# A two-layer decoder trunk: the first layer's first MLP matrix as seven block products over both token halves

## The chip, the cores and the metric

The kernel runs on one core of one Trainium2 chip. The metric is the device time of one execution in microseconds; lower is better. All numbers of the profile come from one profiled execution of the same program.

## The reference

1024 tokens of width 1024 in float32 pass two layers. Layer 0 is an mLSTM (8 heads, chunks of 128 tokens) and an MLP; layer 1 is a latent attention (8 heads, causal, rotary keys and queries) on keys and values that are computed once from the stream after layer 0, and an MLP. Each part is wrapped in two RMS norms and modulated by six vectors that are products of the condition `c` with large matrices. What matters here:

```python
def sqrelu_mlp(h, w1, w2):
    return jnp.square(jax.nn.relu(h @ w1)) @ w2          # w1 (1024, 4096), w2 (4096, 1024)

def rope_tables(positions):
    half = B_ROPE // 2
    inv = ROPE_THETA ** (-jnp.arange(half, dtype=jnp.float32) / half)
    ang = positions.astype(jnp.float32)[..., None] * inv
    return jnp.cos(ang), jnp.sin(ang)
...
        h = modulate(rmsnorm(x, norm_g[l, 2]), sh2, sc2)
        y = sqrelu_mlp(h, mlp_w1[l], mlp_w2[l])
```

## The kernel before

The tokens are handled in two halves of 512 (`hfs[0]`, `hfs[1]`). The stream is kept transposed, features on partitions, so that a block of 128 features and one half is a tile of 128x512. Every float32 product is three matmuls in a reduced format: each operand is split in a high and a low part, and `mm3` (L268) adds low x high, high x low and high x high. For weights, `wload` (L244) reads 512 KB into one of 4 `raw` buffers through SyncE's DMA queue, and `wsplit` (L223) makes the high part with ScalarE (L228) and the low part with VectorE (L229), in two of 8 `ws` buffers. Operands are split in the same way by `split_mod` (L479).

Buffers go by kind: 24 tiles of 128x1024 (`k4`), 8 (`hd`), 8 (`ws`), 4 (`raw`), and smaller ones of 128x512 (3 `tmp`, 6 `tmc`). [...]

*MLP.* `mlp` (from L937) makes a list of steps for one half. A hidden step makes one of 32 blocks of 128 hidden features: 8 k-tiles of `w1`, 24 matmuls of 512 columns, then relu, square and split. An up step multiplies a group of hidden blocks by a part of `w2`, 24 matmuls too, and VectorE adds the result to `y` (`accumulate`). Loads run two steps ahead (`AHEAD`). For the second half of layer 1 alone, pairs of hidden blocks are made by seven block products instead of eight (`hidden_pair`), over the two quarters of that half's tokens.

*Order of the work.* The order is written by hand with generators. `two_streams` runs a dense stream (an MLP) beside another (an attention, or background work): the other yields how many dense steps are to follow; each dense step can also advance a third stream, the background (`fill`), which makes the modulation vectors on VectorE (`ada_chunk`, L374), the rotary tables (`rope_tables`, L1182 and around) and the folded latent weights (`latent_weights`, L1260). Layer 0's MLP of the first half runs beside the second half's norms and this background; that of the second half beside the attention of the first (`mixer1(hfs[0], ...)`, with `attention_first`, which prepares two heads at a time and then attends with them); layer 1's MLP of the first half beside the attention of the second. Before that, `in_turn` weaves a half's output projection (`wout`) with the other half's chunks, and `post` makes the residual and the MLP's input. A scheduler then orders each engine's instructions by the program's priorities, by readiness in its own timeline and by free buffers; at run time each engine's queue is in that order.

The lines that the prediction names: L229, L237 (the adds of `accumulate`), L270 to L272 (`mm3`), L905 (the reload of x for the residual), L926 (its use), L980 (a block sum in `hidden_pair`), L1182 and L1260, L1462 to L1466 (softmax), L301 and L715 (what GpSimd does now).

## Time and profile before

| | |
|---|---|
| median of 3 runs | 2344.38 us (2344.23 to 2345.63) |
| the profiled execution, from first to last instruction | 2341.8 us |
| TensorE busy | 2316.1 us (99%), 12234 matmuls |
| VectorE busy | 1661.9 us (71%) |
| ScalarE busy | 1097.5 us (47%) |
| GpSimd busy | 17.8 us (1%) |
| DMA | 373.02 MB, mean 159 GB/s |

The page gives busy time by engine, the chain of work that ended last, and groups of instructions: line, engine, operation, output and inputs, shapes and count; then busy time in us and mean ns of one; then the engine's idle time ahead of them with what ended it. The view by stretches gives, for a stretch of the span, its length, each engine's busy time with its count, the TensorE clock, the DMA engines' busy share and GB/s. The profiled execution's own time outside the span isn't recorded; the median is 2.6 us above the span.

### The profile page before, as it was taken

To read this page: it belongs to the slowest core of one execution; us is meant where nothing else is said; L and a number is where in the kernel's file an instruction comes from. 1 tells how busy PE (TensorE), PEld (TensorE's weight loads), DVE (VectorE), ACT (ScalarE), POOL (GpSimd) and SP (SyncE) were. 2 spreads that over 40 slices of the span, in tenths; PEclk is the share of its full clock that TensorE was granted. 3 is DMA by queue.
4 is the path that set the end of the run, shared out by engine and by line. 5 is a ranking of instruction groups with operands and counts; after the bars stand their busy time and mean duration, and the time that the engine had idled before them with its cause. 6 is when DMAs were issued, how large, how long until landed. Compare 5 with 4: busy or idle time off the path is not lost.

```text
span 2341.8 us, 32190 instructions
## 1 busy us (share of the span) xinstructions
PE 2316.1 (99%) x12234; PEld 1957.3 (84%) x12234; DVE 1661.9 (71%) x2643; ACT 1097.5 (47%) x1825; POOL 17.8 (1%) x95
## 2 busy tenths in 40 slices
PE   8999999999999999999999999999999999999998
PEld 6888888888888887888888888888888888989997
DVE  6666766868665768777764867765666488788776
ACT  4364335655333454444444554444444444655543
POOL 1000000000000000000000000000000000000000
PEclk9999999999999999999999999999999999999999
DMA  9543454545653845545543454873433452455432
GB/s 319 176 130 121 145 160 142 171 148 167 189 181 114 274 156 167 170 158 179 173 137 119 153 162 154 261 245 132 153 100 129 123 166 81 145 157 163 134 108 108
DMA packets 377595, 373.02 MB, mean 159 GB/s; under 512 B 24323, under 2 KB 284480, under 8 KB 377440
## 3 DMA queue, kind: packets, MB, share of 16 engines
q1 hardware_dynamic: 377152, 370.86, 50.0%
q8 instruction: 96, 1.57, 0.3%
q14 instruction: 59, 0.48, 0.1%
q0 software_dynamic: 288, 0.10, 0.0%
HBM read 312.19 MB, written 58.72 MB: 158 GB/s over the span
## 4 chain that ended last, share of the span: by engine, by line
PE 90%; DVE 4%; DMA 3%; ACT 2%; issue 1%; SPq 0%; DVEq 0%; ACTq 0%
PE ps L270 15%; PE ps L272 15%; PE ps L271 15%; PE pm L270 10%; PE pm L271 10%; PE pm L272 10%; PE pc L270 2%; PE pc L272 2%; PE pc L271 2%; PE pc L1572 1%; DMA raw<-in_mlp_w_dram 1%; PE pm L1458 1%; DVE wl L229 1%; PE pm L812 1%; PE pm L1452 1%
## 5 line engine op out<-in xcount | busy, mean ns | idle before, releaser
L229 DVE TENSOR_TENSOR wl<-raw,wh 128x1024 fp32r<-128x1024 f32 (+3 forms) x367 | 437.9, 1197 | 303.2 <-ACT wh L228 291.9
L228 ACT CAST wh<-raw 128x1024 fp32r<-128x1024 f32 (+3 forms) x367 | 376.8, 1030 | 559.8 <-PE ps L270 218.3
L270 PE MATMUL ps<-k,wl 128*128 128x512 f32 (+1 forms) x1432 | 546.4, 382 | 2.1 <-DVE wl L229 2.1
L272 PE MATMUL ps<-k,wh 128*128 128x512 f32 (+1 forms) x1432 | 539.2, 377 | 0.0
L271 PE MATMUL ps<-k,wh 128*128 128x512 f32 (+1 forms) x1432 | 538.3, 376 | 0.0
L270 PEld LDWEIGHTS ps<-k,wl 128*128 128x128 f32 x1432 | 270.0, 189 | 53.9 <-DVE wl L229 4.0
L272 PEld LDWEIGHTS ps<-k,wh 128*128 128x128 f32 x1432 | 269.7, 188 | 49.4 <-issue 0.2
L271 PEld LDWEIGHTS ps<-k,wh 128*128 128x128 f32 x1432 | 270.1, 189 | 47.8 <-issue 1.4
L237 DVE TENSOR_TENSOR k<-k,pm 128x512 f32<-128x512 f32 (+1 forms) x278 | 226.1, 844 | 81.1 <-PE pm L272 80.4
L270 PE MATMUL pm<-hd,wl 128*128 128x512 f32 x512 | 201.3, 393 | 0.5 <-ACT hd L483 0.5
L271 PE MATMUL pm<-hd,wh 128*128 128x512 f32 x512 | 199.5, 390 | 0.2 <-DVE hd L484 0.2
L272 PE MATMUL pm<-hd,wh 128*128 128x512 f32 x512 | 199.4, 390 | 0.0
L270 PE MATMUL pm<-wh,hd 128*128 128x512 f32 x488 | 193.7, 397 | 4.2 <-ACT raw L1464 2.7
L272 PE MATMUL pm<-wh,hd 128*128 128x512 f32 x488 | 190.6, 390 | 0.0
L271 PE MATMUL pm<-wl,hd 128*128 128x512 f32 x488 | 190.6, 390 | 0.0
L374 DVE SCALAR_TENSOR_TENSOR tma<-raw,cond,tma 128x512 f32<-128x512 f32 x168 | 125.6, 747 | 21.3 <-DMA raw<-in_kv_ada_w_dram 13.4
L1464 ACT ACTIVATE raw<-pm,sm 128x128 f32<-128x128 f32 (+3 forms) x64 | 47.4, 741 | 150.6 <-DVE sm L1463 122.3
L484 DVE TENSOR_TENSOR hd<-tmp,hd 128x512 fp32r<-128x512 f32 x128 | 88.1, 689 | 39.5 <-ACT hd L483 39.0
L270 PEld LDWEIGHTS pm<-hd,wl 128*128 128x128 f32 x512 | 96.2, 188 | 21.2 <-ACT hd L483 0.9
L270 PEld LDWEIGHTS pm<-wh,hd 128*128 128x128 f32 x488 | 91.8, 188 | 26.1 <-ACT raw L1464 5.1
L271 PEld LDWEIGHTS pm<-hd,wh 128*128 128x128 f32 x512 | 96.2, 188 | 20.4 <-DVE hd L484 0.5
L272 PEld LDWEIGHTS pm<-hd,wh 128*128 128x128 f32 x512 | 96.2, 188 | 19.9
(430 smaller groups left out, 3995.4 us busy)
## 6 DMA issues: line engine op xcount, KB each, us to landing
raw<-in_mlp_w_dram SPq DMA_DIRECT2D x256, 512.0 KB, 4.3
raw<-in_ada_w_dram SPq DMA_DIRECT2D x80, 512.0 KB, 4.5
raw<-in_a_w_in_dram SPq DMA_DIRECT2D x44, 512.0 KB, 4.6
xs<-k SPq DMA_DIRECT2D x40, 256.0 KB, 4.5
raw<-in_a_w_out_dram SPq DMA_DIRECT2D x16, 512.0 KB, 5.1
raw<-in_kv_ada_w_dram SPq DMA_DIRECT2D x16, 512.0 KB, 3.9
kd<-k SPq DMA_DIRECT2D x32, 256.0 KB, 3.9
vd<-k SPq DMA_DIRECT2D x32, 256.0 KB, 4.7
```

The source lines that it names most:

```text
L228: nc.scalar.copy(hi[:, :n], r[:, :n])
L229: i = nc.vector.tensor_sub(lo[:, :n], r[:, :n], hi[:, :n].bitcast(F32))
L237: return f(*a, **k)
L270: nc.tensor.matmul(o, ll, rh, start=start, stop=False)
L271: nc.tensor.matmul(o, lh, rl, start=False, stop=False)
L272: pe_last[0] = nc.tensor.matmul(o, lh, rh, start=False, stop=stop)
L374: nc.vector.scalar_tensor_tensor(acc, r[:, kk], cond[:, k : k + 1], acc, ALU.mult, ALU.add)
L484: nc.vector.tensor_sub(lo, u, hi.bitcast(F32))
L812: nc.tensor.matmul(nvs[q][:, r, i], hf.PT[p_][:, r, cs], v[2 * p_ + r], start=g == 0, stop=True,)
L1452: nc.tensor.matmul(o[:, :w], ql, kh, start=True, stop=False)
L1458: nc.tensor.matmul(o[:, :w], qh, kh, start=False, stop=True)
L1464: nc.scalar.activation(pr[:, :n], f, AF.Exp, bias=m, scale=SCALE, accum_out=l)
```

## The change

Layer 0's MLP gets a class of its own, `Mlp`, that works on both halves. `w1` is a 2x2 matrix of blocks (input features 0-511 and 512-1023, hidden features 0-2047 and 2048-4095), the tokens are the two halves; seven block products replace eight. Sixteen pairs of hidden blocks (p, p + 16) go through three sweeps. Sweep 1 makes two products per pair: the first half's hidden block p; one product is stored (`m`). Sweep 2 makes three: the first half's block p + 16; two partial sums are stored (`u`). Sweep 3 makes two: both hidden blocks of the second half. Sweeps 1 and 2 run where the first half's MLP ran, sweep 3 beside the first half's attention. `post` of the second half makes the operands that the block products need, from the first half's MLP input, which is kept in memory (`keep`).

The sums of weight blocks (`t0`) are made early, during layer 0's mLSTM, by `block_sums`: all 16 pairs are in its order; what the steps around it haven't taken by the end of the second half's projections is issued in one block there. The low parts of `w2` are stored when the first half makes them and read back for the second half.

```diff
     def mm3(o, lh, ll, rh, rl, start, stop):
-        nc.tensor.matmul(o, ll, rh, start=start, stop=False)
+        nc.tensor.matmul(o, lh, rh, start=start, stop=False)
         nc.tensor.matmul(o, lh, rl, start=False, stop=False)
-        pe_last[0] = nc.tensor.matmul(o, lh, rh, start=False, stop=stop)
+        pe_last[0] = nc.tensor.matmul(o, ll, rh, start=False, stop=stop)
...
+        def first(self, p_, h):
...
+            def hid(w):
+                pt, c = ps(), tmp()
+                self.product(pt, self.part(w, 0), h)
+                evac(c, pt)
+                nc.gpsimd.dma_start(self.m[p_], c)
+                yield "within"
+                pt, s = ps(), tmp()
+                self.product(pt, self.part(w, 1), h, 4)
+                prompt(nc.vector.tensor_add)(s, c, pt)
+                self.squares(0, p_, s)
...
+        def second(self, p_, ops):
...
+            def hid(ws):
+                s2, w, u = ws
+                u2, u3 = u[:, 0:512], u[:, 512:1024]
...
+                pt = ps()
+                self.product(pt, s2, ops[2])
+                prompt(nc.vector.tensor_add)(u2, u2, pt)
...
+                pt = pc()
+                self.product(pt, self.part(w, 0), ops[3])
+                prompt(nc.vector.tensor_add)(u3, u2, pt)
+                nc.gpsimd.dma_start(self.u[p_], u)
+                yield "within"
+                pt, s = ps(), tmp()
+                self.product(pt, self.part(w, 1), ops[4])
+                prompt(nc.vector.tensor_add)(s, u3, pt)
+                self.squares(0, NPR + p_, s)
...
+        def third(self, p_, ops, buf):
...
+            def hid(ws):
+                w, (u2, u3) = ws
+                pt = ps()
+                self.product(pt, self.part(w, 0), ops[1])
+                with tc.high_priority(PRIO):
+                    nc.vector.tensor_add(u3, u3, pt)
+                    nc.vector.tensor_add(u2, u2, pt)
+                self.squares(1, NPR + p_, u3)
+                yield "within"
+                pt = ps()
+                self.product(pt, self.part(w, 1), ops[0])
+                prompt(nc.vector.tensor_add)(u2, u2, pt)
+                self.squares(1, p_, u2)
...
+        def up_cols(self, half, y, fs, i, last):
...
+            def load():
+                if not half:
+                    w = wload(views, n * P)
+                    nc.gpsimd.dma_start(self.lo[i][:, fs[0] : fs[0] + G], w[1].bitcast(F32))
+                    return w
...
+                for a, f, k in self.runs(fs):
+                    nc.sync.dma_start(rv[:, a : a + k], wcols(w2, i * n * P, n * P, f, k))
+                    nc.sync.dma_start(w[1][:, a : a + k].bitcast(F32), self.lo[i][:, f : f + k])
+                nc.scalar.copy(w[0], rv)
+                return w
...
-            nc.vector.tensor_copy(a, pi)
-            nc.vector.tensor_scalar(a, a, inv, None, ALU.mult)
-            nc.vector.tensor_scalar(kf, a, 1.0 / (2.0 * PI), MAGIC, ALU.mult, ALU.add)
-            nc.vector.tensor_scalar_add(kf, kf, -MAGIC)
+            a, kf, d = tmc(), tmc(), tmc()
+            nc.gpsimd.tensor_copy(a, pi)
+            nc.gpsimd.tensor_scalar(a, a, inv, None, ALU.mult)
+            nc.gpsimd.tensor_scalar(kf, a, 1.0 / (2.0 * PI), MAGIC, ALU.mult, ALU.add)
+            nc.gpsimd.tensor_scalar_add(kf, kf, -MAGIC)
             for part in TWO_PI_PARTS:
-                nc.vector.scalar_tensor_tensor(a, kf, -part, a, ALU.mult, ALU.add)
+                nc.gpsimd.tensor_scalar(d, kf, -part, None, ALU.mult)
+                nc.gpsimd.tensor_add(a, a, d)
                 yield
...
-            nc.vector.tensor_mul(r, r, A.unsqueeze(2).to_broadcast([P, KD, P]))
+            for k in range(KD):
+                nc.scalar.activation(r[:, k], r[:, k], AF.Identity, scale=A[:, k : k + 1])
...
+    order = [*range(1, NPR, 2), *range(0, NPR, 2)][:16]
+
+    def block_sums():
+
+        for p_ in order:
+            a, b = (at_prep[0]()[:, :1024] for _ in range(2))
+            for i, t in enumerate((a, b)):
+                nc.gpsimd.dma_start(
+                    t.rearrange("p (a b) -> p a b", b=P), wcols(mlp_w1[0], (p_ + NPR * i) * P)
+                )
+            yield
+            l_, r_ = slice(0, 512), slice(512, 1024)
+            nc.vector.tensor_add(b[:, r_], b[:, l_], b[:, r_])
+            nc.vector.tensor_sub(b[:, l_], a[:, l_], b[:, l_])
+            nc.gpsimd.dma_start(t0[p_][:, 1024:2048], b)
+            nc.vector.tensor_sub(a[:, l_], b[:, r_], a[:, l_])
+            nc.vector.tensor_sub(a[:, r_], a[:, r_], a[:, l_])
+            nc.gpsimd.dma_start(t0[p_][:, 0:1024], a)
+            yield
...
-    drain(with_bg(gates_in(hfs[0]), bgs, 1))
-    drain(with_bg(qk_last(hfs[0]), bgs, 1))
+    pre = block_sums()
+    at_prep[0] = hd
+    drain(with_bg(with_bg(gates_in(hfs[0]), bgs, 1), pre, 1))
+    drain(with_bg(with_bg(qk_last(hfs[0]), bgs, 1), pre, 1))
     x1 = load_x1()
+    at_prep[0] = k4
+    for _ in range(2):
+        next(pre, None)
...
-    drain(weave_n(with_bg(main, bgs, 1.5), intra0(hfs[1]), 0.95))
+    drain(weave_n(with_bg(with_bg(main, bgs, 1.5), pre, 0.2), intra0(hfs[1]), 0.95))
+    print('LEFT',len(list(pre)))
...
+    two_streams(
+        ms[0].run(ms[0].sweep3(hfs[1], z1, [2] * 8, pair_buf, True)),
+        mixer1(hfs[0], z0, attention_first), bg_rest(),
+    )
```

Also changed: `attention_first` prepares one head's key and query, one pair's rotary query or one pair's values at a time, as a piece beside each round, and attends one head and 256 queries per round with one dense step between rounds; the background in that stage starts with the attention instead of the latent part, at 3 half-steps per dense step; `wout` of layer 1's first half loads two steps ahead; the latent weights are stored through GpSimd's queue; some yields count differently.

More of the change, by code (lines that the diff above doesn't have):

```diff
@@ L217, in mm, with half_op @@
                 mm3(o, w[0][:, ts(k, P)], w[1][:, ts(k, P)], hi[:, k], lo[:, k], k == 0, k == 3)
+    def half_op():
+        t = [k4v(F32R) for _ in range(4)]
+        o = Half()
+        o.hi, o.lo = FH(tiles=t[::2]), FH(tiles=t[1::2])
+        return o
+    class Half:
+        pass
     pace, follow = [None], [False]
@@ L1381, in latent @@
         hf.cq = (his, los)
+        if not hf.i:
+            behind()
         yield 1
@@ L1564, in turned, with attend_beside @@
+    def attend_beside(hf, groups, dense, behind=lambda: None):
         def turned(work):
@@ new lines, in units @@
+        def units():
+            for hh in range(NH):
+                kt, q = keys[hh]
+                if hh == 6:
+                    last_o(hf)
+                p_, r = hh // 2, hh % 2
+                for j in range(2):
+                    yield [((hh, (q, turns[p_][:, r]), kt, values[p_][r]), j)]
+        ahead()
+        yield 0
+        piece()
+        yield 0
+        turn = piece()
+        yield 0.5
+        piece()
+        turn()
+        yield 0.5
+        yield from attend(hf, units(), cycle((1,)), lambda: load_o(hf), 0, piece)
@@ L2178, in go, with two_streams @@
         return r
-    def two_streams(dense, other, fill=iter(()), more=4):
+    def two_streams(dense, other, fill=iter(()), more=3, rest=True):
         traced = nc.cur_bb.bb.instructions
-        at, per = ["hid"], 0
+        at, per, due = "hid", 0, 0
         while True:
@@ L2238, in behind @@
             yield 0.5 if late[0] else 1
-    f0 = mlp(0, hfs[0], z0, [4] * 8)
-    for n in range(20):
-        if next(f0) != "within":
-            next(p1, None)
-    drain(p1)
-    two_streams(f0, behind(bg_latent(), 4))
+    steps, tail = ms[0].sweep1(hfs[0], z0, [4] * 4)
+    f0 = ms[0].run(steps + ms[0].sweep2(hfs[1], z0, [4] * 4, tail))
+    for v in f0:
+        if v != "within" and next(p1, end) is end:
+            break
+    two_streams(f0, behind(bg_latent(), 5))
     rope_perm()
@@ L2275, with beside @@
     u1 = FH(claim=True)
+    def beside(dense, fill):
+        v = None
+        while (d := go(dense)) is not end:
+            if v != "last" and d != "within":
+                v = next(fill)
     def all_out():
@@ L2286 @@
     fill = all_out()
-    v = None
-    dense = mlp(1, hfs[1], u1, [2] * 6 + [4] * 5, True, True)
-    while (d := go(dense)) is not end:
-        if v != "last" and d != "within":
-            v = next(fill)
+    beside(mlp(1, hfs[1], u1, [2] * 6 + [4] * 5, True, True), fill)
     drain(fill)
```

530 lines of the change are left out of this document (487 added, 43 removed).

## The prediction

> **What bounds the kernel now.** I read the page's header and first part, then its chain, then the groups of one dense stretch, then busy time by stage.
>
> ```profile
> span 2341.8 us, 32190 instructions
> PE 2316.1 (99%) x12234; PEld 1957.3 (84%) x12234; DVE 1661.9 (71%) x2643; ACT 1097.5 (47%) x1825; POOL 17.8 (1%) x95
> PE 90%; DVE 4%; DMA 3%; ACT 2%; issue 1%; SPq 0%; DVEq 0%; ACTq 0%
> ```
>
> TensorE is busy 2316.1 of 2341.8 us and holds 90% of the chain that ended last. Only 25.7 us of it is idle, so the time can fall noticeably only if matmuls go. A busy TensorE is modelled from overlapping matmuls, so what one matmul costs has to be counted. The stretch from 700 to 800 us, in the first layer's MLP, has it never idle (this row is of the view by stretches; columns: length, then busy time and count of each engine, clock, DMA share, GB/s):
>
> ```profile
> 700.00:800.00 100.00, 100.00 (x444) 82.34 (x443) 65.41 (x99) 37.28 (x51) 0.00 (x0) 1.00 0.53 163
> ```
>
> The groups of that stretch:
>
> ```profile
> L271 PE MATMUL pm<-hd,wh 128*128 128x512 f32 x75 | 29.2, 390 | 0.0
> L272 PE MATMUL pm<-hd,wh 128*128 128x512 f32 x74 | 28.8, 390 | 0.0
> L270 PE MATMUL pm<-hd,wl 128*128 128x512 f32 x74 | 28.8, 390 | 0.0
> L270 PE MATMUL ps<-k,wl 128*128 128x512 f32 x72 | 28.6, 397 | 0.0
> L272 PE MATMUL ps<-k,wh 128*128 128x512 f32 x72 | 28.1, 390 | 0.0
> L271 PE MATMUL ps<-k,wh 128*128 128x512 f32 x72 | 28.1, 390 | 0.0
> L1270 PE MATMUL pc<-ident,tma 128*128 128x128 f32 x5 | 1.4, 270 | 0.0
> ```
>
> 439 matmuls of 512 columns and 5 small ones fill 100 us. With the small ones at 0 to 0.27 us each, a large one costs 0.2246 to 0.2278 us; I take 0.226, not the 0.39 of its modelled span.
>
> **The change, part by part.**
>
> *Products.* The first MLP matrix of layer 0 now takes, for both halves, 64 hidden blocks of 8 k-tiles and 3 matmuls: 1536. After, each of 16 pairs takes 2 + 3 + 2 block products of 4 k-tiles and 3 matmuls: 1344. So 192 go, at 0.226 us: **-43.4 us** (43.1 to 43.7). The second matrix, the attention's scores, transposes and products, and layer 1 keep their counts. A dense step of 24 matmuls is 5.42 us.
>
> *Stages.* Work moves: sweeps 1 and 2 (1728 matmuls where the first half's MLP has 1536) run beside the background vectors, and only sweep 3 (1152, 384 fewer) stays beside the attention. The present stages, MLP of the first half, then three parts of MLP of the second half with the attention:
>
> ```profile
> 447.00:841.00 394.00, 393.99 (x1750) 324.87 (x1749) 275.34 (x375) 176.57 (x236) 0.55 (x4) 1.00 0.55 172
> 841.00:955.00 114.00, 112.81 (x514) 92.29 (x513) 93.46 (x135) 57.52 (x89) 0.41 (x2) 1.00 0.55 173
> 955.00:1244.00 289.00, 287.63 (x1479) 242.41 (x1478) 209.00 (x358) 128.52 (x230) 3.24 (x18) 1.00 0.51 159
> 1244.00:1350.00 106.00, 105.38 (x460) 86.04 (x458) 76.66 (x93) 51.07 (x72) 0.39 (x4) 1.00 0.46 148
> ```
>
> VectorE's prices, from groups of the whole run (the first) and of 447 to 841 us:
>
> ```profile
> L980 DVE TENSOR_TENSOR raw<-raw,raw 128x512 f32<-128x512 f32 x16 | 11.0, 685 | 0.0
> L229 DVE TENSOR_TENSOR wl<-raw,wh 128x1024 fp32r<-128x1024 f32 x76 | 92.0, 1222 | 62.6 <-ACT wh L228 62.6
> L237 DVE TENSOR_TENSOR k<-k,pm 128x1024 f32<-128x1024 f32 x28 | 34.1, 1217 | 23.8 <-PE pm L272 23.8
> L1182 DVE SCALAR_TENSOR_TENSOR tmc<-tmc,tmc 128x512 f32<-128x512 f32 x14 | 9.6, 686 | 0.1
> L1260 DVE TENSOR_TENSOR raw<-raw,mods 128x1024 f32<-128x1024 f32 x6 | 7.3, 1225 | 0.2
> ```
>
> Sweeps 1 and 2 add 64 sums from PSUM (43.8 us at 0.685), 16 more half-size weight splits (11.0), and 36 more operations on operands (52 for 16, +24.7); the rotary chain (9.6) and the latent weights' product (7.3) leave VectorE. 275.3 + 79.5 - 16.9 = 338 us in 394 + 43 = 437: from 70% to 77%. In the attention's stage 48 weight splits go (-58.7; the second half's w2 takes its low part from memory), 24 accumulations (-29.2) go and 48 sums come (+32.9): 379 becomes 324 us, while the stage shrinks by 384 x 0.226 = 87 to 422: from 74% to 77%. So neither stage is VectorE-bound on average, and I cost these edits at nothing, TensorE being the cover. Within the attention the cover is thinner. One pair of heads now:
>
> ```profile
> 1032.00:1104.00 72.00, 71.25 (x374) 60.13 (x372) 55.07 (x95) 30.83 (x57) 0.82 (x4) 1.00 0.53 169
> L1462 DVE TENSOR_REDUCE sm<-pm 128x1 f32<-128x384 f32 (+3 forms) x8 | 3.8, 479 | 1.1 <-PE pm L1458 1.1
> L1466 DVE TENSOR_SCALAR raw<-raw,sm 128x384 f32<-128x384 f32 (+3 forms) x8 | 3.1, 383 | 0.1
> L1464 ACT ACTIVATE raw<-pm,sm 128x384 f32<-128x384 f32 (+3 forms) x8 | 4.2, 527 | 16.6 <-DVE sm L1463 10.0 <-issue 6.6
> ```
>
> (The first row is of the view by stretches, the others are groups of that stretch.) Eight dense steps per pair become four, 72 us becomes 50. VectorE gives up 8 splits, 8 accumulations and 4 splits of hidden blocks (22.3 us) and gets about 9.5: 42.3 of 50.3 us, 84%, with the background beside it. Between scores and transposes stands one step of 5.4 us and a piece of projections of up to 3.4 (15 matmuls); the softmax itself, reduce, exponential and scale, is 1.4 us by these rows, twice, partly overlapped. It fits unless three or more queued operations of 1.2 us come first. Bounds: nothing, and 2.5 us in each of 16 rounds (40 us); I take **+5 us**, near the present 1 us a pair, as one round in five misses.
>
> *Early block sums.* 16 pairs, four operations of 0.685 us each: 43.8 us of VectorE, before 447 us. Its load there:
>
> ```profile
> 300.00:350.00 50.00, 50.00 (x352) 43.06 (x351) 33.87 (x82) 17.59 (x37) 0.00 (x0) 1.00 0.53 150
> 350.00:400.00 50.00, 50.00 (x269) 41.14 (x269) 30.54 (x68) 25.87 (x51) 0.10 (x1) 1.00 0.49 152
> 400.00:447.00 47.00, 47.00 (x209) 38.57 (x208) 38.53 (x53) 29.48 (x45) 0.69 (x7) 1.00 0.57 178
> ```
>
> By the loops, 15 of the 32 half-steps are taken on the way and 17 are issued in one block, ahead of the second half's output chain. At that point the 24 k4 buffers hold 8 for h, 4 for q and k, 4 for v, 8 for the first half's o: all of them. The first that come free now are taken by the reloaded x (of the view by tile):
>
> ```profile
> L905 SPq DMA_DIRECT2D k<-xt x4: 460/496/644, 383.0 to 384.6; - x4
> L926 DVE TENSOR_TENSOR hd<-hd,k x8: 683/685/686, 410.3 to 416.4; 128x512 f32<-128x512 f32 x8
> raw<-in_mlp_w_dram SPq DMA_DIRECT2D x256, 512.0 KB, 4.3
> ```
>
> Eight and a half pairs want 17 buffers, and being earlier in the program they go first from 383 us on. Their sums alone are 8.5 x 2.74 = 23 us on a VectorE that is 82% busy from 400 us. In the best case they find gaps (0); taken four pairs at a time, two rounds of load and store at the 4.3 us of that row plus the sums are 2 x 8.6 + 23 = about 41 us, past the 27 us that x has between load and use; 14 us late. Some is hidden under the second half's output projection, some repeats in the sigmoid gates that want the same buffers; I take **+12 us**.
>
> *Rotary tables and the GpSimd queue.* 36 elementwise operations of 128x512 (18 per half) go to an engine of which this trace shows, as nearest rows,
>
> ```profile
> L715 POOL MEMSET tmc<- 128x512 f32 x2 | 1.1, 528 | 72.6 <-PE pc L625 72.6
> L301 POOL DMA_DIRECT2D raw<-in_norm_g_dram x1 | 0.7, 702 | 0.3 <-issue 0.3
> ```
>
> A memset only writes, so 0.53 us is the lower end; twice VectorE's 0.686 is my upper end: 19 to 49 us in all. VectorE's clamp waits for the end of each chain, and behind the chain in GpSimd's queue stand the stores of w2's low parts and of the partial sums, whose buffers (8 ws, 3 tmp) the weight splits wait for. With five half-steps of background per dense step the chain is paced near its own speed. Bounds 0 and 38 us (below, the first rival); I take 1 us each, and **+6 us**.
>
> *Traffic.* In MB: early sums read 17 and written 17, partial sums written and read 8 and 17, low parts 34, the kept operand 4, first-matrix loads 4 fewer: about 92 more. Here are the present total and a dense stretch, in which TensorE loses 0.01 us at 332 GB/s against some 200 to come on average (465 MB in 2320 us):
>
> ```profile
> DMA packets 377595, 373.02 MB, mean 159 GB/s; under 512 B 24323, under 2 KB 284480, under 8 KB 377440
> ...
> 800.00:820.00 20.00, 19.99 (x88) 16.26 (x87) 12.98 (x14) 8.63 (x11) 0.00 (x0) 1.00 0.94 332
> ```
>
> So I cost it at nothing; without that cover a step would wait for its load, up to the 4.3 us above. *High part first* in every triple lets TensorE start before the low part is made; the present wait for it is the 2.1 us here:
>
> ```profile
> L270 PE MATMUL ps<-k,wl 128*128 128x512 f32 (+1 forms) x1432 | 546.4, 382 | 2.1 <-DVE wl L229 2.1
> ```
>
> **-2 us.** The sum on the span: 2341.8 - 43.4 + 5 + 12 + 6 - 2 = 2319.4. The median 2344.4 is 2.6 above the profiled span; with that, 2322.
>
> **The rivals.**
>
> *The rotary chain takes VectorE with it.* If the two engines exclude each other while GpSimd works on two inputs, 49 us of GpSimd time is 49 us that VectorE's two-input operations lose; at 77% load it can absorb 11, and TensorE waits 38. 2344.4 - 43.4 + 38 = 2339, with the other terms up to 2350. For: nearly all VectorE rows above read two buffers. Against: the chain comes in short pieces. [...]
>
> *The softmax shows.* 1.5 to 2.5 us per round in 16 rounds, 24 to 40 us: 2325 to 2341 without the other terms. For: 84% load and half the cover. Against: the present pairs, at 76%, lose under 1 us each.
>
> *Slower: the block sums hold the buffers.* If the pairs go one after another (load 4.3, sums 2.74, store 4.3: 11.3 us), 8.5 of them take 96 us from 383, and the residual of the first half, which wants its x by 410, comes some 69 us late, with sweep 1 behind it; with the gates' wait, up to 83. 2344.4 - 43.4 + 69 = 2370, to 2384. It decides from about 13 us after x's present use plus the saving: when the last buffer comes back after some 440 to 455 us. Against: 8 buffers free at once allow four pairs together.
>
> *All hidden.* Nothing added: 2299. That fewer products are made than said can be excluded: the counts are written out.
>
> **How the numbers follow.** The forecast, 2305 to 2334 (4 to 33 us of added waits where the sum has 21), has 0.5; all hidden 0.07; the rotary lock 0.11; the softmax 0.12; slower 0.20. The range 2297 to 2374 leaves out the far end of the slower case and little below. A measurement of this kernel can tell about 0.2% (4.7 us) from no change: 2340 to 2349 gets 0.07 from the upper ends of the two middle rivals, slower 0.21, faster 0.72.
>
> **What would show it.** Right: 12042 matmuls; VectorE near 1713 us (1661.9 + 43.8 + 62.6 - 55); sweeps 1 and 2 with TensorE idle under 10 us in 437; attention pairs of 50 to 52 us; the reloaded x issued between 383 and 400 us. Wrong: TensorE idle in a block after 383 us (block sums), around the GpSimd operations with VectorE waiting for them (lock), or before the transposes in each round (softmax); or a pitch other than 0.226 us in the sweeps.

## The result and the profile after

The changed kernel takes 2381.07 us in the median of 4 runs (2375.67 to 2381.46), the kernel before 2344.59 beside it: a ratio of 1.015, 95% interval 1.0135 to 1.0164. It is 36.5 us slower where the forecast was 22 us faster, and it lies above the range.

The page of the changed kernel, header, first part and chain:

```profile
span 2379.6 us, 32796 instructions
PE 2298.5 (97%) x12042; PEld 1932.3 (81%) x12042; DVE 1709.8 (72%) x2771; ACT 1128.1 (47%) x1913; POOL 160.7 (7%) x271
PE 66%; DVE 7%; DMA 5%; ACT 3%; issue 2%; SPq 1%; DVEq 0%; POOL 0%; ACTq 0%; POOLq 0%
```

The 192 matmuls are gone, and TensorE's share of the chain fell from 90% to 66%: it now waits all over the kernel, for VectorE and for loads. Two numbers of the forecast came out as said, VectorE's 1709.8 us (1713 was said) and the matmuls.

Where it waits is read from stretches. The view by stretches (length, then busy time and count of PE, PEld, DVE, ACT, POOL; clock, DMA share, GB/s), first of the kernel before, then of the changed one:

```profile
0.00:50.00 50.00, 41.97 (x259) 30.00 (x260) 31.50 (x71) 22.42 (x37) 6.66 (x27) 1.00 0.96 335
50.00:100.00 50.00, 49.99 (x315) 43.88 (x314) 31.85 (x55) 15.83 (x34) 0.53 (x1) 1.00 0.56 185
...
550.00:700.00 150.00, 150.00 (x677) 124.33 (x676) 104.40 (x140) 59.03 (x75) 0.00 (x0) 1.00 0.61 188
1000.00:1250.00 250.00, 248.63 (x1271) 209.49 (x1271) 176.55 (x294) 107.99 (x189) 2.83 (x16) 1.00 0.50 156
```

```profile
0.00:50.00 50.00, 37.29 (x241) 26.42 (x241) 30.09 (x70) 19.71 (x33) 14.23 (x33) 0.96 1.01 335
50.00:100.00 50.00, 41.93 (x216) 36.15 (x217) 28.00 (x41) 12.31 (x28) 9.13 (x18) 0.84 0.92 320
350.00:400.00 50.00, 44.52 (x276) 36.67 (x275) 32.32 (x81) 15.23 (x35) 11.01 (x15) 0.93 0.74 223
450.00:500.00 50.00, 45.65 (x192) 36.47 (x191) 45.75 (x63) 35.19 (x55) 1.29 (x9) 0.97 0.88 278
...
550.00:700.00 150.00, 139.41 (x600) 111.60 (x599) 137.84 (x168) 69.83 (x95) 68.50 (x60) 0.98 0.78 258
1000.00:1250.00 250.00, 228.91 (x1186) 190.93 (x1185) 177.41 (x354) 109.37 (x215) 3.69 (x18) 0.97 0.64 203
```

Four places lose. In the first 50 us the DMA engines were at a share of 0.96 already; now they are at 1.01, and at 0.92 instead of 0.56 in the next 50. At 350 to 400 and 450 to 500 us, around the block of early sums, 5.5 and 4.4 us of TensorE go (before, by the rows of the prediction, nothing there). From 550 to 700 us VectorE is busy 137.84 of 150 us and TensorE loses 10.6. From 1000 to 1250 us, beside the attention, TensorE loses 21 us although VectorE is as busy as before (177.41 us against 176.55).

A busy TensorE can also be stretched (by the sums below the changed kernel loses 136.0 us, where 81.1 of its span are idle), so I add the losses up from the starts of the matmuls: for each, the time to the next start less the median of that time for the same operands in the kernel before (at most 0.23 us). Sums by stage, in us; stages end at 100 us, at the first load of layer 0's output matrix, at the first relu of its MLP, at the latent part, at the attention's first and last weights, and at the second half's latent part:

| kernel | to 100 | projections | block, chunks | sweeps or MLP | latent | attention | behind it | rest | all |
|---|---|---|---|---|---|---|---|---|---|
| before | 18.6 | 5.8 | 0.3 | 1.8 | 0 | 8.7 | 2.3 | 17.1 | 54.7 |
| changed | 34.5 | 11.6 | 14.9 | 17.8 | 0.4 | 35.0 | 6.1 | 15.8 | 136.0 |

81.3 us more are lost. The sum of the medians, which is what the matmuls would take back to back, fell from 2276.0 to 2233.5, by 42.5. Together that is +38.8, against +37.8 between the two spans. So the gain of the products came in full, and four losses of 15 to 26 us (the start with the projections, the block, the sweeps, the attention) took it back twice.

### The profile page after: what moved, and what is told of

The parts are those of the page before. It is cut to its first block, busy times and chain, and to the rows that moved or that the text cites. A ratio compares the mean times of both kernels' runs of the same rounds, so it can differ in the third digit from the quotient of the medians.

```text
span 2379.6 us, 32796 instructions
## 1 busy us (share of the span) xinstructions
PE 2298.5 (97%) x12042; PEld 1932.3 (81%) x12042; DVE 1709.8 (72%) x2771; ACT 1128.1 (47%) x1913; POOL 160.7 (7%) x271
## 4 chain that ended last, share of the span: by engine, by line
PE 66%; DVE 7%; DMA 5%; ACT 3%; issue 2%; SPq 1%; DVEq 0%; POOL 0%; ACTq 0%; POOLq 0%
PE ps L282 10%; PE ps L280 10%; PE ps L281 10%; PE pm L280 8%; PE pm L281 8%; PE pm L282 8%; PE pc L281 2%; PE pc L282 2%; PE pc L280 2%; DMA raw<-in_mlp_w_dram 2%; DVE tma L384 1%; PE pc L2023 1%; DVE wl L239 1%; DMA raw<-in_ada_w_dram 1%; DVE k L247 1%
## 5 line engine op out<-in xcount | busy, mean ns | idle before, releaser
L238 ACT CAST wh<-raw 128x1024 fp32r<-128x1024 f32 (+5 forms) x323 | 327.9, 1017 | 490.3 <-PE ps L281 170.3
L239 DVE TENSOR_TENSOR wl<-raw,wh 128x1024 fp32r<-128x1024 f32 (+5 forms) x323 | 383.2, 1188 | 242.2 <-ACT wh L238 198.5
L280 PE MATMUL ps<-k,wh 128*128 128x512 f32 (+1 forms) x1228 | 466.9, 380 | 5.5 <-ACT k L682 1.7
L282 PE MATMUL ps<-k,wl 128*128 128x512 f32 (+1 forms) x1228 | 460.1, 375 | 2.0 <-DVE wl L239 2.0
L281 PE MATMUL ps<-k,wh 128*128 128x512 f32 (+1 forms) x1228 | 459.8, 374 | 0.0
L280 PEld LDWEIGHTS ps<-k,wh 128*128 128x128 f32 x1228 | 232.0, 189 | 50.4 <-issue 2.6
L282 PEld LDWEIGHTS ps<-k,wl 128*128 128x128 f32 x1228 | 231.9, 189 | 45.0 <-DVE wl L239 3.4
L281 PEld LDWEIGHTS ps<-k,wh 128*128 128x128 f32 x1228 | 232.1, 189 | 40.9 <-issue 1.7
L282 PE MATMUL pm<-wh,hd 128*128 128x512 f32 x488 | 190.4, 390 | 0.0
L384 DVE SCALAR_TENSOR_TENSOR tma<-raw,cond,tma 128x512 f32<-128x512 f32 x168 | 131.9, 785 | 17.0 <-DMA raw<-in_ada_w_dram 11.9
L280 PEld LDWEIGHTS pm<-wh,hd 128*128 128x128 f32 x488 | 91.7, 188 | 24.8 <-ACT raw L1834 4.5
L282 PEld LDWEIGHTS pm<-wh,hd 128*128 128x128 f32 x488 | 91.6, 188 | 19.7 <-DVE hd L494 0.5
L280 PE MATMUL pc<-k,wh 128*128 128x256 f32 (+1 forms) x316 | 103.4, 327 | 3.9 <-DVE hd L494 3.9
L281 PEld LDWEIGHTS pm<-wl,hd 128*128 128x128 f32 x488 | 91.7, 188 | 18.4 <-issue 0.5
L280 PE MATMUL pm<-hd,wk 128*128 128x512 f32 x256 | 101.6, 397 | 2.2 <-ACT hd L493 2.2
L281 PE MATMUL pc<-k,wh 128*128 128x256 f32 (+1 forms) x316 | 103.4, 327 | 0.2 <-DVE k L494 0.2
L282 PE MATMUL pc<-k,wl 128*128 128x256 f32 (+1 forms) x316 | 103.2, 327 | 0.0
L281 PE MATMUL pm<-hd,wk 128*128 128x512 f32 x256 | 101.0, 395 | 1.9 <-DVE hd L494 1.9
```

The lines of the kernel that those rows point to most:

```text
L238: nc.scalar.copy(hi[:, :n], r[:, :n])
L239: i = nc.vector.tensor_sub(lo[:, :n], r[:, :n], hi[:, :n].bitcast(F32))
L280: nc.tensor.matmul(o, lh, rh, start=start, stop=False)
L281: nc.tensor.matmul(o, lh, rl, start=False, stop=False)
L282: pe_last[0] = nc.tensor.matmul(o, ll, rh, start=False, stop=stop)
L384: nc.vector.scalar_tensor_tensor(acc, r[:, kk], cond[:, k : k + 1], acc, ALU.mult, ALU.add)
```

## The experiments

Medians stand beside the kernel before in the same series (2343.45 to 2346.34); ratios are to it, with 95% intervals. A difference from the changed kernel's 2381.07 is one between two series, and the kernel before moves by up to 2.9 us from one to another; set against its own series, a gain named below is mostly about 1 us smaller. "Loss" is a column of the table above.

**Where the early sums lose.** `no_sums` makes all 16 pairs' sums in sweep 2:

```diff
-    order = [*range(1, NPR, 2), *range(0, NPR, 2)][:16]
+    order = [*range(1, NPR, 2), *range(0, NPR, 2)][:0]
```

> No block sum is made early; all 16 pairs' sums are made in sweep 2. After against before, TensorE loses about 20 us more up to 150 us of the span, 14 more from 340 to 500, 17 more from 540 to 700 and 33 more from 950 to 1260. Theory 1 (each loss belongs to the part of the change that stands there): the first two go, 34 us, and sweep 2 takes the sums into its idle VectorE time: about 2347. Rival (VectorE and the loads are what is short, wherever the sums stand): 44 us of sums and 8 MB more of loads in sweep 2 give back 15 to 30: 2362 to 2377.

Measured 2356.34, ratio 1.0045 (1.0028 to 1.0061): 24.7 us better than the changed kernel, between theory and rival. `no_block` cuts the order at 7, so that none is left for the block:

> Seven pairs early instead of 16, so that nothing is left to be issued in one block ahead of the output projections; nine pairs' sums are made in sweep 2. Theory 1: the 14 us between 340 and 500 us of the span go, the rest stays: about 2367. Rival: nine pairs in sweep 2 give back as much: 2375 to 2381.

Measured 2368.37, 1.0104 (1.0089 to 1.0119), and the block's loss is 1.3 instead of 14.9. `no_start` leaves the first five pairs out of the start:

```diff
-    drain(with_bg(with_bg(gates_in(hfs[0]), bgs, 1), pre, 1))
-    drain(with_bg(with_bg(qk_last(hfs[0]), bgs, 1), pre, 1))
+    drain(with_bg(gates_in(hfs[0]), bgs, 1))
+    drain(with_bg(qk_last(hfs[0]), bgs, 1))
```

(and the order ends at 11).

> No pair's sums in the gates and the last query and key blocks (the start); 11 pairs later, most of them in the block, five in sweep 2. Theory 1: the 20 us up to 150 us go: about 2361. Rival (the start is slower for another reason, such as the high part first in each triple): about 2381.

Measured 2356.70, 1.0056 (1.0036 to 1.0077): the first two columns fall from 34.5 and 11.6 to 17.9 and 6.7. So the start costs 21.5 us by the columns (24.4 by the medians) and the block 13.6 (12.7). Without any early sums the sweeps lose 27.9 instead of 17.8, which is why `no_sums` gains less than the two together.

How the start loses is in the transfers from 30 to 80 us (queue: packets, MB, share; then issues with median us to landing), before and after:

```profile
q1 hardware_dynamic: 8300, 12.57, 73.0%
...
raw<-in_a_w_in_dram SPq DMA_DIRECT2D x6, 512.0 KB, 5.0
```

```profile
q1 hardware_dynamic: 5188, 8.53, 50.7%
q0 software_dynamic: 2291, 8.37, 48.5%
...
hd<-in_mlp_w_dram POOLq DMA_DIRECT2D x10, 512.0 KB, 10.1
...
raw<-in_a_w_in_dram SPq DMA_DIRECT2D x2, 512.0 KB, 22.1
```

GpSimd's queue takes half of the DMA engines' work (48.5% beside 50.7%), though the sums that it is there for are first read at 684 us, and the weights that TensorE waits for land in 22.1 us instead of 5.0. In `no_start` they land in 5.4 us. The waits from 30 to 110 us show the end of it:

```profile
ACT wh L238 <- DMA raw<-in_a_w_in_dram: 26.6, 6, 15.2
...
PE ps L280 <- ACT k L247: 7.7, 1, 7.7
```

(before: 5.8 us for the same load; in `no_start` 8.5). In the block it is the order on VectorE: from the timeline of VectorE (start, us, instruction, idle time before),

```profile
391.43 0.69 DVE L2583 TENSOR_TENSOR k<-k 128x512 f32<-128x512 f32 x1 [1.39 <-DMA k<-in_mlp_w_dram]
392.04 0.68 DVE L858 TENSOR_TENSOR tmc<-pm,sm 128x512 f32<-128x512 f32 x1
```

and of the waits from 370 to 500 us

```profile
PE pc L884 <- DVE tmc L858: 5.5, 1, 5.5
```

a block sum that waits 1.39 us for its load stands ahead of L858, which TensorE needs for a chunk, and four more block sums of 0.69 us each stand in the queue in the 4.3 us before it; without the block that wait is 0.5 us. From 450 to 465 us TensorE waits 2.7 and 1.7 us for ScalarE, which works without a gap there; whether the block sums set that isn't shown.

**The rotary tables.** `rot_vector` has the chain on VectorE again.

> The rotary tables back on VectorE, all else as after. GpSimd's 28 operations took 1.4 to 1.7 us each there, 55 us with the rest, in the stretch in which TensorE loses 17 us. If they hold VectorE up: 10 to 17 us less, 2364 to 2371. Rival (that stretch is short of VectorE for the background and the new sums): the 13 us return to VectorE and the time stays or grows by some us: 2379 to 2390.

Measured 2374.41, 1.0127 (1.0112 to 1.0143): 6.7 us better (5.5 set against its own series), between theory and rival. While GpSimd is at the chain, 577 to 668 us of the changed kernel, VectorE's groups are (busy, mean ns)

```profile
L384 DVE SCALAR_TENSOR_TENSOR tma<-raw,cond,tma 128x512 f32<-128x512 f32 x34 | 31.9, 939 | 1.3 <-DMA raw<-in_ada_w_dram 0.7
L239 DVE TENSOR_TENSOR wl<-raw,wh 128x1024 fp32r<-128x1024 f32 x15 | 21.2, 1415 | 1.4 <-ACT wh L238 1.3
L247 DVE TENSOR_TENSOR k<-k,pm 128x1024 f32<-128x1024 f32 x7 | 8.4, 1210 | 0.9 <-PE pm L282 0.9
...
L382 DVE TENSOR_SCALAR tma<-raw,cond 128x512 f32<-128x512 f32 x4 | 4.1, 1023 | 0.0
L366 DVE TENSOR_REDUCE sm<-pc 128x4 f32<-128x512 f32 x4 | 2.7, 679 | 0.9 <-PE pc L364 0.9
```

against these before, 566 to 687 us:

```profile
L374 DVE SCALAR_TENSOR_TENSOR tma<-raw,cond,tma 128x512 f32<-128x512 f32 x42 | 31.5, 750 | 0.6
L229 DVE TENSOR_TENSOR wl<-raw,wh 128x1024 fp32r<-128x1024 f32 x22 | 26.9, 1223 | 25.1 <-ACT wh L228 25.1
L237 DVE TENSOR_TENSOR k<-k,pm 128x1024 f32<-128x1024 f32 x11 | 13.4, 1218 | 9.2 <-PE pm L272 9.2
...
L356 DVE TENSOR_REDUCE sm<-pc 128x4 f32<-128x512 f32 x5 | 3.4, 685 | 0.0
L372 DVE TENSOR_SCALAR tma<-raw,cond 128x512 f32<-128x512 f32 x5 | 2.4, 478 | 0.0
```

Two inputs from SBUF take 939 instead of 750 ns and 1415 instead of 1223, the one-input multiply 1023 instead of 478; an add with one input from PSUM (1210 against 1218) and the reduction (679 against 685) don't change. With the chain on VectorE (`rot_vector`, the same stretch) the three are back at 749, 1222 and 479 ns, so it is GpSimd's work beside them that made them longer. The rows with two inputs from SBUF are longer, as the prediction's rival has it; the one-input multiply, which that rival leaves out, is longer too. That the two engines exclude each other isn't shown. The price here is small: the groups of L384, L239 and L382 grow by 34 x 0.19 + 15 x 0.19 + 4 x 0.55, some 11.5 us of VectorE, a quarter of the 49 us that the rival took. Where the 6.7 us end up isn't settled: from 550 to 700 us TensorE is only 0.5 us busier without GpSimd (139.93 against 139.41), and from 700 to 950 us it is never idle in either. So most of the gain lies outside the stage of the chain.

**Sweeps 1 and 2.** At 5 half-steps of background per dense step (the kernel before has 4) VectorE is at 92% from 550 to 700 us and at 71 from 700 to 800. `rate3` and `rate4` change only that pace:

```diff
-    two_streams(f0, behind(bg_latent(), 5))
+    two_streams(f0, behind(bg_latent(), 3))
```

> Only the pace of the background beside sweeps 1 and 2 is changed: 3 half-steps per dense step instead of 5, so the same background is spread over more of the two sweeps. Theory (VectorE is full for 50 to 150 us at the pace of 5 and empty-handed later): the 16 us that TensorE lost in the sweeps beyond the kernel before fall to about 5, and the time goes from 2381 to about 2368; VectorE's busy share in 550 to 600 us falls from 99% to about 85%. Rival (the sweeps are held by loads or buffers that their own 3 products per pair need): the sweeps still lose about 16, 2376 to 2383. If the spread background runs out of room before the sweeps end, part moves to the attention and the time rises.

> Background beside sweeps 1 and 2 at 4 half-steps per dense step. At 3 the stretch 550 to 700 us lost 2.9 us of TensorE instead of 10.6, but the background outlasted the sweeps and ran bare for some 33 us. At 4 it ends, by the order of the program, with 18 of the sweeps' dense steps and half-steps left (22 at 5). Theory (local saturation of VectorE at the pace of 5): 550 to 700 us lose 4 to 8, nothing runs bare, and the time is 3 to 7 us below 2381. Rival (what was won in 550 to 700 us at the pace of 3 came from something else, as the other contents of these steps): 550 to 700 us still lose 10, 2379 to 2383.

Measured 2408.24, 1.026 (1.0243 to 1.0278), and 2384.53, 1.0172 (1.015 to 1.0193). The stretches of `rate3`:

```profile
550.00:700.00 150.00, 147.12 (x651) 120.64 (x650) 123.08 (x145) 74.02 (x101) 70.36 (x61) 1.00 0.70 231
900.00:950.00 50.00, 17.30 (x59) 12.09 (x58) 31.77 (x71) 28.32 (x62) 7.11 (x12) 0.62 0.66 225
```

With VectorE at 82% TensorE loses 2.9 instead of 10.6; but the background no longer fits beside the sweeps, and its last part runs bare for 33 us. At 4 it fits, and the loss from 550 to 700 us is 20 (the row: PE 130.23), with VectorE at 85%. So VectorE's busy share does not order the losses. Stretches of 50 us say the same, two of the changed kernel and one of `rate4`:

```profile
550.00:600.00 50.00, 48.16 (x213) 39.00 (x212) 49.76 (x64) 27.23 (x40) 23.08 (x19) 1.00 0.60 200
650.00:700.00 50.00, 43.49 (x184) 34.05 (x183) 42.70 (x53) 21.34 (x27) 13.54 (x14) 0.97 0.90 302
...
600.00:650.00 50.00, 37.87 (x161) 30.70 (x160) 38.16 (x46) 15.87 (x21) 30.77 (x25) 0.90 0.73 244
```

With VectorE full TensorE loses 1.8 us; with VectorE at 85% and the DMA engines at 0.90 it loses 6.5; with VectorE at 76% it loses 12.1. The waits of `rate4` from 500 to 900 us name where TensorE stood:

```profile
PE pc L364 <- DVE tma L384: 18.8, 5, 8.6
```

The four transposes that close a modulation vector stand in TensorE's queue ahead of dense work and wait for the vector's last multiply-add. `rate4_pend` and two kernels without early sums issue them two loads later:

```diff
+            if q == 1 and pending:
+                yield from pending.pop()
...
+        if later[0]:
+            pending.append(ada_turn(acc, bias, dst))
+            return
```

> As the run at 4 half-steps per dense step (2384.5), but in the sweeps the transposes that close a modulation vector are issued two loads into the next one instead of right behind its last multiply-add; the sums alternate between two buffers. Theory (transposes too early in TensorE's queue; TensorE waited 18.8 us for them in 500 to 900 us at this pace, 3.4 at 5): the sweeps' loss of 28 falls to about 10 and the time to 2364 to 2369. Rival (VectorE itself is late, and the next consumer waits in the transposes' place): the sweeps still lose over 22, 2379 to 2386.

> No early block sums (all 16 pairs summed in sweep 2) and the background at 4 half-steps per dense step. If the two add up: 2356 less 3 to 7, about 2351. If sweep 2's own sums fill VectorE at 4 as well (its sweeps lost 28 at the pace of 5), 2354 to 2358.

> The same edit without early block sums (2368 before the edit, 24.5 us of the transposes' waits). Theory: 2344 to 2350. Rival (VectorE full with sweep 2's own sums): 2358 or more.

> The same at 5 half-steps per dense step, without early block sums (2356 before the edit, with only 3.8 us of the transposes' waits). Theory: 2350 to 2356, as little of its loss was that. Rival: the shift moves other work too, over 3 us either way beyond that.

Measured 2387.49, 1.0184 (1.0169 to 1.0199); 2368.23, 1.0097 (1.0082 to 1.0113); 2367.47, 1.0099 (1.0084 to 1.0114); 2363.87, 1.0088 (1.0073 to 1.0103). My theory fell: at the pace of 4 the transposes' waits fall from 18.8 to 9.8 us, and from 24.5 to 7.8 without early sums, at 5 they grow from 3.8 to 15.1; other consumers wait in their place, and no time is won. The transposes are one place where the lateness shows, not the reason. With the sums of sweep 2 on top the sweeps lose 28 to 46. In the changed kernel, from 550 to 700 us, SyncE's queue waits 85 us for VectorE's weight splits and background sums to give `raw` buffers back before it can load, which fits a VectorE that is behind but doesn't show it to be the cause. Nor are the block products needed for such a loss: `old_mlp` below, with eight products and no block sums at the pace of 5, loses 29 us here, where the kernel before loses 1.8.

**The attention.** Five kernels. `bg_early` moves all of its background to the sweeps (at the pace of 3). `bg_narrow` keeps its loads and instructions, on 16 of 512 columns, and so leaves out most of these sums. `g1_early` moves a quarter to the sweeps' end. `cover` gives the rounds 1.5 and 1 dense steps in turn. `old_mlp` has the old MLP of layer 0 beside the new attention. Parts of the five edits, in this order:

```diff
-        mixer1(hfs[0], z0, attention_first), bg_rest(),
+        mixer1(hfs[0], z0, attention_first),
...
-                            acc, r[:, kk], cond[:, k : k + 1], acc, ALU.mult, ALU.add
+                            acc[:, :n], r[:, kk, :n], cond[:, k : k + 1], acc[:, :n], ALU.mult, ALU.add
...
-        mixer1(hfs[0], z0, attention_first), bg_rest(),
+        mixer1(hfs[0], z0, attention_first), bg_rest((SH2, SC2, G2)), 3,
...
-        yield from attend(hf, units(), cycle((1,)), lambda: load_o(hf), 0, piece)
+        yield from attend(hf, units(), cycle((1.5, 1)), lambda: load_o(hf), 0, piece)
...
-        ms[0].run(ms[0].sweep3(hfs[1], z1, [2] * 8, pair_buf, True)),
+        mlp(0, hfs[1], z1, [2] * 14 + [4]),
```

> No background beside the attention: all of it (also layer 1's last four modulation vectors) runs beside sweeps 1 and 2, at 3 half-steps per dense step. Theory A (attention lost 35 us because the background's VectorE work and its loads stand in the queues ahead of the softmax): attention's loss falls from 35 to about 10 and the time to about 2350, if the sweeps bear the added work; if they don't, the loss moves to the sweeps, which then lose 30 or more. Theory B (one dense step between rounds and the added pieces are too thin a cover by themselves): attention still loses about 30, and the time stays within 2370 to 2385.

> In the attention stage the background's multiply-adds work on 16 of 512 columns (this leaves most of the sums of layer 1's modulation vectors out); its loads, buffers and number of instructions are unchanged. Theory A1 (the VectorE time of the background delays the softmax): some 60 us of VectorE go from that stage, attention's loss falls from 35 to 10 to 15 and the time to 2355 to 2362. Theory A2 (its loads and buffers, or the place of waiting instructions in VectorE's queue): the loss stays near 30, 2375 to 2382. Theory B (thin cover): stays near 30 too; the run without background in this stage tells A2 and B apart.

> One of layer 1's four last modulation vectors (16 of 64 background steps of the attention stage) is made at the end of sweep 2, where VectorE has about 15 of 50 us free; everything else as in the changed kernel. Theory (background beside the attention costs about 20 of its 35 us, in proportion to its amount): attention loses about 30, the sweeps no more than 2 further, and the time is 2374 to 2379. Rival (any background at all spoils the rounds, or the last dense steps of sweep 2 have no room): 2380 to 2390.

> The attention's rounds get 1.5 and 1 dense steps in turn instead of 1 each; the 7 more come out of those beside the residual and norm behind the attention (10 of 17 are left there). Background as in the changed kernel. Theory (the cover of one dense step is too thin for the softmax with the background in VectorE's queue): the attention stage loses 15 to 25 instead of 35, the stage behind it some 5 more, and the time is 2365 to 2378. Rival (the waits are for loads, which come no earlier): attention still loses 32 or more, 2380 to 2390.

> Layer 0's MLP is the one of the kernel before again (eight products, 12234 matmuls, no block sums, no stored partial sums), with the new attention of one head per round, the new order of pieces and the rotary tables on GpSimd kept. Theory B (the attention's new form is what loses): attention still loses 25 to 35 us against 9 of the kernel before, and the time is 2362 to 2372. Rival (sweep 3's stream, with its four loads and more sums per pair, is what loses): attention loses 9 to 15, and the time is 2343 to 2352.

`old_att` puts the old form, two heads per round, beside sweep 3:

> The changed kernel with the attention of the first half in its old form (two heads prepared and attended per round), beside sweep 3. The attention then uses 8 dense steps more, so none is left for the residual and norm behind it. Theory (the form of one head per round is what loses with the background beside it): the attention stage loses 10 to 18 us instead of 35, the stage behind it 20 to 40 instead of 6, 2372 to 2395. Rival (sweep 3's stream loses): the attention stage still loses 30 or more, 2395 to 2415.

| kernel | median us | ratio (95%) | attention's loss |
|---|---|---|---|
| bg_early | 2447.48 | 1.043 (1.0414 to 1.0446) | 14.3 (sweeps 106) |
| bg_narrow | 2365.77 | 1.0084 (1.0069 to 1.0099) | 21.9 |
| g1_early | 2378.64 | 1.0133 (1.0112 to 1.0154) | 32.9 |
| cover | 2395.84 | 1.0216 (1.0201 to 1.0232) | 36.5 (behind it 21) |
| old_mlp | 2401.03 | 1.0232 (1.0216 to 1.0247) | 34.9 (sweeps 29) |
| old_att | 2428.50 | 1.0363 (1.0346 to 1.038) | 45.2 (behind it 45) |

In the ten runs above, which leave this stage's work as it is (at most the sums are read from another place), its loss is 26 to 38: differences under 6 us can't be read here, so g1_early tells nothing. The background counts: without it 14, with a small part of its VectorE time 22. The cover doesn't: more dense steps between the rounds left 36.5. Nor is sweep 3's stream needed for it: the old MLP beside the new attention loses the same. My theory of thin cover falls, and that the old form would lose little beside sweep 3 fell too.

What the three kernels that lose some 35 (the changed one, cover, old_mlp) share stood in the waits of SyncE's queue. Before, from 955 to 1200 us, the stores of outputs, keys and values waited

```profile
SPq L1593 <- ACT tmp L1592: 8.4, 9, 1.1
SPq L1514 <- ACT k L483: 2.6, 3, 0.9
```

and in the changed kernel, 977 to 1255 us,

```profile
SPq L1974 <- ACT tmp L1973: 39.2, 9, 9.7
SPq L2132 <- ACT k L493: 26.8, 4, 8.7
SPq L2102 <- ACT k L493: 24.0, 7, 8.8
```

With smaller rows that is 97 us against 14, in old_mlp 107. The kernel before has the same kinds of stores; it is the new form of the attention that makes them wait so long: with the old form beside sweep 3 (`old_att`) they wait 24 us. The weight loads and background loads that are issued later stand behind them in the same queue: in one case nothing is issued there from 1136.41 us on, a store of outputs waits 7.8 us for its copy on ScalarE and is issued at 1144.26, and the next weight load follows at 1144.69. ScalarE's casts then wait for loads (in this stage of the changed kernel)

```profile
ACT wk L1223 <- DMA raw<-in_mlp_w_dram: 13.4, 7, 3.0
ACT wh L238 <- DMA raw<-t: 12.2, 4, 6.2
```

and the softmax's exponentials are behind the casts. One case, from the timeline of ScalarE and then of TensorE (start, us, instruction, idle time before):

```profile
1139.52 1.05 ACT L1223 CAST wk<-raw 128x1024 fp32r<-128x1024 f32 x1 [1.88 <-DMA raw<-in_mlp_w_dram]
...
1141.66 0.67 ACT L1834 ACTIVATE raw<-pm,sm 128x512 f32<-128x512 f32 x1
```

```profile
1143.66 1.12 PE L1942 MATMUL pc<-ident,raw 128*128 128x128 f32 x4 [3.00 <-DVE raw L1836]
```

A cast of the MLP waits 1.88 us for its load, two activations of the MLP follow it, then the exponential, VectorE's scale, and TensorE's transposes are 3.0 us late. `store` moves these stores to other queues:

```diff
-                        nc.sync.dma_start(oT[ts(u.hh, P), ts(u.j, 256)], o)
+                        nc.scalar.dma_start(oT[ts(u.hh, P), ts(u.j, 256)], o)
...
-                nc.sync.dma_start(kd[hh, i, :, ts(hf.i, H)], kt[:, i].bitcast(F32))
+                nc.gpsimd.dma_start(kd[hh, i, :, ts(hf.i, H)], kt[:, i].bitcast(F32))
...
-                    nc.sync.dma_start(
+                    nc.gpsimd.dma_start(
```

> The changed kernel with the first half's attention storing keys and values through GpSimd's queue and its outputs through ScalarE's, instead of SyncE's. Theory (stores that wait for their data stand in SyncE's queue ahead of loads: 97 of 277 us in this stage, against 14 in the kernel before; weight casts then wait for the loads in ScalarE's queue, ahead of the softmax's exponentials): SyncE's waits for stores go, the attention's loss falls from 35 to 20 or less, and the time to 2360 to 2367. Rival (a load that starts earlier waits for its buffer instead, and the slower landing of GpSimd's stores holds buffers): the loss stays over 30, 2376 to 2384.

Measured 2366.01, 1.0094 (1.008 to 1.0108): 15 us better, the loss is 21.1. The stretch of `store` that answers to 228.91 of 250:

```profile
1000.00:1250.00 250.00, 237.85 (x1254) 199.37 (x1253) 189.27 (x365) 115.64 (x221) 24.51 (x52) 0.99 0.68 216
```

TensorE makes 68 more matmuls in the same 250 us. SyncE's queue waits as long as before the edit in all (some 187 us against 183, by the rows of the view), now for free buffers (23.3 us for VectorE's split in the longest row). What fell is the time that ScalarE's weight casts wait for loads, from 39.5 to 20.6 us. The two kernels with the stores moved lose 21 and 22 us in this stage, the changed one and the ten runs above 26 to 38, so 4 to 17 us of it are the stores'. Of the changed kernel's stores of 256 KB, `m` through GpSimd's queue lands in 4.8 us (median), `vd` and `kd` through SyncE's in 3.7 and 4.2.

**What helped, together.** `ns_store_rot`: no early sums, stores moved, rotary tables on VectorE.

> No early block sums (2356), the stores of the attention on the other queues as in the run beside it, and the rotary tables on VectorE again. If the parts add up: 2356 less 12 to 18 for the stores, less 0 to 7 for the rotary tables, 2331 to 2344, at or below the kernel before. If the stores' place was not what held the loads: 2349 to 2356.

Measured 2339.58 (11 runs, 2337.34 to 2345.18), ratio 0.9982, interval 0.9973 to 0.9991: 4.9 us faster than the kernel before, with losses of 18.1, 7.6, 0.7, 25.7, 0.4, 22.3, 5.7 and 15.7. So the seven products can pay, barely: 96.2 us of loss still stand against 54.7. The kernel before with its own stores moved wasn't run, so how much of the 4.9 us is the products' isn't shown.

## Why the prediction was wrong, step by step

Three terms of the sum failed: the attention's (+5, measured 26), the sweeps' (nothing, 16) and the traffic's (nothing, 21 to 24).

- **Products, -43.4 us.** Right: 12042 matmuls, 42.5 us less back to back.
- **Attention, +5.** Failed in size: 26 us (8.7 to 35.0). It was worked out from the softmax's own operations and the cover of a dense step. VectorE's busy share, by which I judged it, was lower than I said (177.41 of 250 us is 71%, against 77% for the stage and 84% for a pair). The step left out SyncE's queue: stores that wait for their data stand there ahead of the loads. Moving them took 14 us off the loss (35.0 to 21.1) and 15 off the time; taking the background away took 21 off the loss. The two aren't separate prices: bg_early still has 92 us of waits for stores and loses 14. A held queue may cost only where the background's loads and sums fill the time that would make up for it: bg_narrow, with 79 us of such waits, all of those loads and few of the sums, loses 22, which fits but doesn't settle it.
- **Sweeps 1 and 2, nothing.** Failed: 16 us. The mean was right (324.83 us of VectorE in the 421 us from 513 to 934, 77%), and no argument for a loss of nothing: it falls in 150 us in which VectorE is at 92%. The sum also left out that the pace went from 4 to 5. The cause stays open: in the same stretch a pace of 3 lost 2.9 us, of 5 10.6 and of 4 20, and the old MLP at the pace of 5 loses 29 in its stage.
- **Early block sums, +12.** The block costs 12.7 by no_block: right in size, in part by luck, as the mechanism was partly another. The reloaded x was late (415 to 447 us, not 383 to 400), but 5.5 us are one queue: block sums, one of which waits for its load, stand on VectorE in front of work that TensorE needs.
- **Traffic, nothing.** Failed: 21 to 24 us at the start, by no_start. The row at 332 GB/s came from a stretch whose loads run two steps ahead. The first 50 us were at a DMA share of 0.96 before the change; that row was left out, and from 30 to 80 us GpSimd's queue got half of the engines (48.5% beside 50.7%).
- **Rotary tables, +6.** 6.7 by rot_vector, which agrees by luck as far as the runs show: TensorE is only 0.5 us busier in the stage of the chain. GpSimd's 36 operations took 55 us, above my 19 to 49. VectorE's two-input operations were longer (939 against 750 ns, 1415 against 1223), as the rival said, but at a quarter of its price.
- **High part first, -2.** Not borne out: L282, now last, waits 2.0 us for the low part, as L270 did (2.1). No run has the old order with all else as changed.
- **The rivals.** The time lies in the interval of the slower one (2370 to 2384), but its mechanism, buffers held by the block, is worth 12.7 of the 36.5 us and not 69. By its own terms (5, 12 and -2) the rotary rival's upper end is 2354, not the 2350 that I wrote. I gave each rival one place to lose; the change had four, each of which I had priced at 0 to 12.

Still open are the cause of the sweeps' loss; what holds the old form of attention beside sweep 3 (33 us in its first 290; its casts wait 33.1 us for the loads of sums); and the remaining 22 us of the attention and 26 of the sweeps in the best kernel.

## What to carry to other kernels

A moved step is priced on every queue that it issues on: a store that waits for its data holds the loads behind it on that queue (97 us of such waits in the attention against 14), which no busy share shows; the waits of the DMA queues do. "Free" traffic is priced from the row of that very stretch: here a second queue had 48.5% of the engines' time and left the first 50.7 instead of 73.0, though nobody waited for its data, and the weights landed in 22.1 us instead of 5.0. And a mean share of 77% says nothing about 150 us at 92%: ask for the stretches in which new work lands, and for the waits there, as the busy share alone didn't order the losses.

## What was unexpected of the hardware

On GpSimd a multiply of 128x512 float32 by a constant took longer than an add of two tiles (of the groups by form, changed kernel, with VectorE at work beside it):

```profile
L1548 POOL TENSOR_SCALAR tmc<-tmc 128x512 f32<-128x512 f32 x14 | 24.3, 1739 | 2.1 <-DVE k L494 1.0
L1549 POOL TENSOR_TENSOR tmc<-tmc,tmc 128x512 f32<-128x512 f32 x14 | 19.6, 1398 | 0.7
```

Both lie above my bounds of 0.53 to 1.37 us. An instruction that multiplies by one constant and adds another (L1545) took 634 ns, twice: two operations in one were far shorter than the 1739 of one alone. And of the five groups of VectorE above the one-input multiply by a column grew most with GpSimd beside it, 1023 against 478 ns, and 479 in rot_vector.
